# Conditioning products of a first block on TensorE instead of GpSimd, in a two-block transformer kernel on Trainium2

## The chip, the cores and the metric

The kernel runs on one core of one Trainium2 chip. The metric is the device time of one execution in microseconds. Three runs are shown, and their median is what a change is compared with.

## The reference

256 tokens of width 1024 go through two blocks. Both are modulated by conditioning vectors, a product of one activated vector with a wide matrix:

```python
silu_c = jax.nn.silu(c)
mod_lat = jnp.split((silu_c @ w_mod[l] + b_mod[l])[:, None, :], N_MOD, axis=-1)
h_lat = rmsnorm(x, norm_mix_g[l]) * (1 + mod_lat[1]) + mod_lat[0]
mix_lat, mix_ctx = token_mixer(h_lat, h_ctx, ...)
x = x + mod_lat[2] * mix_lat
h_lat = rmsnorm(x, norm_ffn_g[l]) * (1 + mod_lat[4]) + mod_lat[3]
x = x + mod_lat[5] * moe_ffn(h_lat, ...)
...
c_act = jax.nn.silu(c)
mod = c_act @ w_ada[l] + b_ada[l]
shf, scf = jnp.split(c_act @ w_ada_f + b_ada_f, 2, axis=-1)
```

`w_mod` and `w_ada` are 1024 x 6144 in float32, `w_ada_f` is 1024 x 2048. Block 1's `token_mixer` projects the 256 tokens and 256 context tokens with `w_in` (1024 x 9280), runs a gated linear recurrence over both directions (8 heads of 128) and an attention with compressed keys (8 heads), and merges the two through gates. An expert layer follows (32 experts, the best four per token, about 400 MB of weights). Block 2 has another recurrence, a gated scan, a hierarchical expert layer and the last norm. All is float32.

## The kernel before

One core does everything in one program. Weights come from HBM in tiles of 128 x 2048 float32 (1 MB, `wload`, L293). In block 1 a tile of projection weights `w` is split by `wsplit` (L542) into two float32r parts: a cast on ScalarE (`wsh`, L538) and a subtraction on VectorE (`wsl`, L539), in halves of 1024 columns. `mm3` (L548) then multiplies split weights with split activations `hs` in three passes (L551 to L553) into PSUM tiles `tp`, `fp` or `pf`.

TensorE's work is a list of items `self.q`. An item has `prep()`, which issues its weight loads and splits, and `run()`, a generator that issues a few products and yields their time. `step` (L494) prepares the first two items and advances the first; `fill(us)` (L512) steps for so many microseconds, `need` steps until an item is done. The chain of the recurrence for a pair of heads (`chain`, L752) is a generator that issues its own steps on VectorE, ScalarE and TensorE (`gram`, `st`, `av`) and, after each, `fill`s with items: the projections of the next pair of heads. There are four pairs; beside the fourth come the query and key projections, and then the eight gate projections `g8s` (L900). Instructions of one engine run in the order in which the program ends up placing them, and a load is issued where its ring has a slot.

The conditioning vectors are handled as 28 rows of 512 values, and their results are kept in `rowall` (128 x 128; value 128g + i of row r is on partition 32g + r, column i). The four rows that block 1's first norm needs are made on TensorE at the start (`mod_first`, L362): for each of 8 blocks of 128 channels and each of 4 column blocks, a matmul with 32 weight columns (`cpad`, in which the column of row r holds the activated vector and the others zeros) writes 32 partitions of `modps`, a VectorE instruction adds it to `rowall`, and a transpose (`modT`) turns it into columns.

The next twenty rows, `MODS1` (8 of `w_mod`, 12 of `w_ada`), run on GpSimd beside the projections (`pool_mods`, L404). GpSimd issues their loads itself, into two slots of a ring of their own (`wm`). For each half of a row's matrix:

```python
nc.gpsimd.tensor_mul(w4, w4, self.cs[:, c + 4 * a:c + 4 * a + 4, None].to_broadcast([128, 4, 512]))
nc.gpsimd.tensor_add(w[:, 0:1024], w[:, 0:1024], w[:, 1024:2048])
```

and then 512-column sums into `macc` (L434 to L437). `tick` (L476) advances this by one step per `PACE1` = 2800 ns of accounted TensorE work, and 5000 ns after a row's last sum `reduce` (L416) has TensorE add up the partitions: four matmuls against a one-hot column (`mr`, L419), and a VectorE addition to `rowall` (L421). `end_mods` (L442) finishes whatever is left as block 1 ends. The four rows of `w_ada_f` are made later, in block 2, on TensorE by `mod` (L346). `mod_cols` (L396) and `bcast_rows` (L450) turn rows into columns or spread them over partitions.

Of the kernel before, what the change touches and what calls it, by code (L numbers as in the profile page):

```python
# [21 lines left out]
PACE1 = 2800  # L22
MODS1 = [(1, j) for j in range(4, 12)] + [(2, j) for j in range(12)]
NWS, NU, NV = 8, 32, 20
NWR, NWM = 3, 2
# [42 lines left out]
def shape_consts():  # L68
# [16 lines left out]
    c['fconst'] = np.ascontiguousarray(np.concatenate([ident, perm, tri, cosT, sinT, iota], 1))  # L85
# [21 lines left out]
def layout(i):  # L107
# [3 lines left out]
    for n, k in VECS:  # L111
# [13 lines left out]
    d['bmods'] = np.ascontiguousarray(np.concatenate([mix, i['b_mod'][0][2048:], i['b_ada_2'][0], i['b_ada_f_2'], mix])  # L125
                                      .reshape(32, 4, 128).transpose(1, 0, 2).reshape(128, 128))
# [36 lines left out]
class Item:  # L163
    """a piece of work for the tensor engine: prep() starts its loads, run(weights) yields the time of each step"""
# [6 lines left out]
class Router:  # L171
    """logits of x's rows, normed and modulated, as x's columns come in: r * (x @ (A w)) + (B @ w + b)"""
# [17 lines left out]
    def cols(self, j):  # L190
        """columns 256 j .. 256 j + 255 are there"""
# [22 lines left out]
    def finish(self, lgt):  # L214
        """lgt[b]: where the logits go; returns 1 / root mean square of the rows"""
# [10 lines left out]
class Ker:  # L226
# [9 lines left out]
    def run(self):  # L236
        with ExitStack() as es:
            tc = self.tc
            self.cp = es.enter_context(tc.tile_pool(name="const", bufs=1))
            self.wp = es.enter_context(tc.tile_pool(name="wts", bufs=NWM))  # L240
            self.sm = es.enter_context(tc.tile_pool(name="small", bufs=2))
            self.pp = es.enter_context(tc.tile_pool(name="psum", bufs=8, space=PSUM))
            self.q, self.lags, self.side, self.sums = [], [], None, []
            own = self.own = [(self.wp, "w"), (self.wp, "wm")]
# [8 lines left out]
            else:  # L253
# [4 lines left out]
                for _ in self.pool_mods([(2, j) for j in range(12)] + [(3, j) for j in range(4)], lambda n: self.cp.tile([128, 512], F32, name=n, tag=n)):  # L258
                    self.drain()
                self.tick(6000)  # L260
# [7 lines left out]
            if self.start <= 1:  # L268
                with tc.tile_pool(name="moe1", bufs=1, side="right", reuse_waits="tile") as p, tc.tile_pool(name="w2", bufs=NW2, reuse_waits="tile") as wp2, tc.tile_pool(name="w2x", bufs=NW2X, reuse_waits="tile") as wp3:
                    self.wq = own[1:] * 2 + own[:1] * 3 + [(wp3, "w")] * NW2X + [(wp2, "w")] * NW2  # L270
                    self.moe1(p, route, (wp2, "w"))
# [7 lines left out]
            with tc.tile_pool(name="moe2", bufs=1, reuse_waits="tile") as p, tc.tile_pool(name="w2b", bufs=NW2B, reuse_waits="tile") as wp2:  # L279
                self.wq = own[1:] * 2 + own[:1] * 3 + [(wp2, "w")] * NW2B  # L280
# [5 lines left out]
    # ---- helpers  # L286
# [6 lines left out]
    def wload(self, src, n=WCOL, slot=None, eng=None):  # L293
        pool, tag = slot or self.wq[self.wi % len(self.wq)]
        t = pool.tile([128, WCOL], F32, name="w", tag=tag, bufs=NWR if tag == "w" and pool is self.wp else None)
# [8 lines left out]
    def consts(self):  # L304
# [3 lines left out]
        fc = cp.tile([128, 1152], F32, name="fc")  # L308
        nc.scalar.dma_start(fc[:, 0:128], d['fconst'][:, 0:128])
        self.fc_rest = lambda: nc.sync.dma_start(fc[:, 128:], d['fconst'][:, 128:])  # L310
        self.ident, self.perm, self.tri = fc[:, 0:128], fc[:, 128:256], fc[:, 256:384]
        self.cosT, self.sinT, self.iota = fc[:, 384:640], fc[:, 640:896], fc[:, 896:1152]
# [4 lines left out]
        # conditioning vectors: columns for the products with w_mod, w_ada  # L317
# [6 lines left out]
        # views [:, 31-r:63-r] have the filled columns in r and, for the second conditioning, 28+r  # L324
# [4 lines left out]
        self.onehot = cp.tile([128, 63], F32, name="onehot")  # L329
        nc.gpsimd.memset(self.onehot, 0.0)  # L330
        nc.gpsimd.memset(self.onehot[:, 31:32], 1.0)
        # chunks of conditioning vectors: row r's 128 columns of group g on partition 32g+r; biases to begin with
        self.rowall = cp.tile([128, 128], F32, name="rowall")
        nc.scalar.dma_start(self.rowall, d['bmods'])
# [7 lines left out]
    def msrc(self, which, j):  # L342
        src, r, c = {1: ('wmod', j, 0), 2: ('wada', 12 + j, 16), 3: ('wadaf', 24 + j, 16)}[which]
        return [self.d[src][2 * j + a] for a in range(2)], r, c

    def mod(self, which, j, cpad):  # L346
        """work item: a chunk of the conditioning vectors, c@W[:, 512j:512j+512]"""
        nc = self.nc
        src, r, _ = self.msrc(which, j)
# [12 lines left out]
    def mod_first(self, q, tile):  # L362
        """channels 256 q .. 256 q + 255 of block 1's first shift and scale, of both conditionings"""
        nc = self.nc

        def run(ws):
            ps = self.ps("modps")
            for k in range(8):
                for g in range(4):
                    w = ws[g // 2]  # L370
                    w, o = (w[k // 2], 256 * (k % 2)) if isinstance(w, list) else (w, 256 * k)
                    o += 128 * (g % 2)
                    nc.tensor.matmul(ps[32 * g:32 * g + 32, :128], self.cpad1[:, k, 31 - q:63 - q], w[:, o:o + 128],
                                     start=(k == 0), stop=(k == 7))
                yield 210
            nc.vector.tensor_add(self.rowall, self.rowall, ps[:, :128])
            pt = self.ps("modT")
            nc.tensor.transpose(pt[:, :128], self.rowall, self.ident)
            for i, r in enumerate((q, 28 + q)):
                nc.vector.tensor_copy(self.mcol1[:, i, :16].rearrange("p (s k) -> p s k", s=2)[:, :, 2 * q:2 * q + 2],  # L380
                                      pt[:, :128].rearrange("p (s g r) -> p s g r", s=2, g=2)[:, :, :, r])

        def load():
            ws = []
            for s in range(2):
                src = self.d['wmix'][4 * s + q]
                if 2 * q + s < 3:
                    ws.append(self.wload(src, slot=self.own[1 if q == 0 else 0]))
                    continue
# [5 lines left out]

    def mod_cols(self, *todo):  # L396
        """rows to columns: (first row, number, destination [128, 4 n])"""
        nc = self.nc
        pt = self.ps("modT")
        nc.tensor.transpose(pt[:, :128], self.rowall, self.ident)  # L400
        for r, n, dst in todo:
            nc.vector.tensor_copy(dst.rearrange("p (j g) -> p g j", g=4), pt[:, :128].rearrange("p (g r) -> p g r", g=4)[:, :, r:r + n])

    def pool_mods(self, todo, acc_tile):  # L404
        """the same on GpSimd, a step at a time beside the tensor engine's work, which then sums the partitions"""
        nc = self.nc
        slot = (self.wp, "wm")
        loads = [(w, j, a) for w, j in todo for a in range(2)]

        def load(i):  # L410
            if i < len(loads):
                w, j, a = loads[i]
                return self.wload(self.msrc(w, j)[0][a], slot=slot, eng=nc.gpsimd)
# [1763 lines left out]
```

## Time and profile before

| | us |
|---|---|
| runs | 2249.55, 2257.85, 2250.76 |
| median of the runs | 2250.76 |
| profiled execution, first to last instruction (span) | 2246.4 |
| between that span and the median | 4.4 |
| TensorE (PE) busy | 2001.8 (89%) |
| VectorE (DVE) busy | 1133.6 (50%) |
| ScalarE (ACT) busy | 530.4 (24%) |
| GpSimd (POOL) busy | 436.1 (19%) |

The profiled execution is listed with its span alone; its own time is not told apart from the runs'. Block 1 takes the first 645 us or so, its experts the next 1000, and block 2 the rest. In the rows further down, PE is TensorE, DVE VectorE, ACT ScalarE, POOL GpSimd, SP the engine that issues loads. A group of instructions reads: line, engine, operation, output and input by the program's names, their shapes, count | busy time in us, mean ns of one | idle time ahead of them and what ended it.

### The profile page before, as it was taken

What the parts mean: (1) busy time and instruction counts of PE and PEld (TensorE: products, weight loads), DVE (VectorE), ACT (ScalarE), POOL (GpSimd) and SP (SyncE); (2) the same over time, 40 slices, a digit from 0 to 9 for tenths busy, and PEclk for the clock granted to TensorE, in tenths of its full rate; (3) what the DMA queues carried; (4) which work ended last, traced back from release to release, by engine and by line L of the source; (5) the groups of instructions that cost most, each with busy time, mean ns of one, the idle gap of its engine ahead of it and who ended that gap; (6) DMA issues with size and microseconds to landing.
All of it is one profiled execution on the core that took longest, in us unless ns stands there. A gap on an engine that the chain in (4) does not pass through costs nothing. (4 is left out here: it accounts for less than half of the span.)

```text
span 2246.4 us, 31459 instructions
## 1 busy us (share of the span) xinstructions
PE 2001.8 (89%) x13205; PEld 1202.1 (54%) x13206; DVE 1133.6 (50%) x1766; ACT 530.4 (24%) x925; POOL 436.1 (19%) x245
## 2 busy tenths in 40 slices
PE   6578779889989999998999999999969998898996
PEld 4467668776674333333333333333348998765653
DVE  5987998997552323333332424233368564321223
ACT  3233335424341000000000100000035633221112
POOL 1754755996300000000000000000032201000000
PEclk9698989989999999998999999999979999899998
DMA  8333424554369999999999999999942236799992
GB/s 340 120 124 130 136 100 151 187 199 167 132 256 374 417 418 416 419 410 387 416 418 418 416 416 417 417 416 418 373 179 99 77 120 257 262 367 337 363 357 78
DMA packets 172908, 646.11 MB, mean 288 GB/s; under 512 B 11508, under 2 KB 78068, under 8 KB 125524
## 3 DMA queue, kind: packets, MB, share of 16 engines
q1 hardware_dynamic: 165216, 600.84, 68.9%
q0 software_dynamic: 5760, 41.95, 5.3%
q8 instruction: 108, 1.77, 0.3%
q10 hardware_dynamic: 1780, 1.20, 0.2%
q14 instruction: 44, 0.36, 0.0%
HBM read 642.89 MB, written 1.05 MB: 287 GB/s over the span
## 5 line engine op out<-in xcount | busy, mean ns | idle before, releaser
L1307 PE MATMUL gu<-w,gT 128*64 128x512 f32 x2048 | 480.8, 596 | 0.0
L1307 PEld LDWEIGHTS gu<-w,gT 128*64 128x64 f32 x2048 | 147.6, 137 | 277.0 <-issue 260.3
L539 DVE TENSOR_TENSOR wsl<-w,wsh 128x1024 fp32r<-128x1024 f32 (+1 forms) x141 | 242.6, 1735 | 46.5 <-ACT wsh L538 46.3
L1338 PE MATMUL y<-w,aT 128*64 128x512 f32 x1024 | 229.7, 600 | 0.1
L1774 POOL MEMSET cpad<- 128x504 f32 x1 | 0.5, 517 | 1059.5 <-DVE x L1239 1059.5
L538 ACT CAST wsh<-w 128x1024 fp32r<-128x1024 f32 (+1 forms) x141 | 143.7, 1028 | 209.2 <-PE tp L552 150.9
L1317 DVE TENSOR_SCALAR act<-gu 128x256 f32<-128x256 f32 x64 | 27.2, 425 | 310.6 <-PE gu L1376 307.3
L1222 DVE SCALAR_TENSOR_TENSOR ylo<-y,sw,yhi 128x512 fp32r<-128x512 f32 x64 | 48.1, 751 | 254.0 <-ACT yhi L1221 254.0
L429 POOL TENSOR_TENSOR w<-w,cs 128x2048 f32<-128x2048 f32 x40 | 154.7, 3867 | 25.6 <-DMA w<-in_wmod_dram 14.8
L553 PE MATMUL tp<-hs,wsl 128*128 128x256 f32 (+1 forms) x424 | 143.6, 339 | 11.8 <-DVE wsl L539 11.7
L1338 PEld LDWEIGHTS y<-w,aT 128*64 128x64 f32 x1024 | 72.9, 138 | 148.1 <-issue 143.3
L551 PE MATMUL tp<-hs,wsh 128*128 128x256 f32 (+1 forms) x424 | 149.9, 353 | 0.2 <-DVE sg L898 0.2
L552 PE MATMUL tp<-hs,wsh 128*128 128x256 f32 (+1 forms) x424 | 142.5, 336 | 0.0
L1481 PE MATMUL ab<-w,gT 128*64 128x256 f32 x1024 | 127.7, 385 | 0.0
L1221 ACT ACTIVATE yhi<-y,sw 128x512 fp32r<-128x512 f32 x64 | 44.0, 687 | 293.4 <-PE y L1376 239.7
L431 POOL TENSOR_TENSOR w<-w 128x1024 f32<-128x1024 f32 x40 | 109.2, 2732 | 2.8
L1238 DVE TENSOR_TENSOR gated<-co,gtb 128x512 f32<-128x512 f32 x128 | 88.4, 690 | 33.7 <-PE co L1233 26.3
L1319 ACT ACTIVATE sge<-act 128x512 f32<-128x512 f32 x32 | 20.2, 631 | 351.0 <-DVE act L1317 351.0
L553 PEld LDWEIGHTS tp<-hs,wsl 128*128 128x128 f32 x424 | 89.8, 212 | 19.3 <-DVE wsl L539 13.4
L1481 PEld LDWEIGHTS ab<-w,gT 128*64 128x64 f32 x1024 | 76.4, 137 | 39.1 <-issue 8.3
L551 PEld LDWEIGHTS tp<-hs,wsh 128*128 128x128 f32 x424 | 90.2, 213 | 7.7 <-issue 2.7
L552 PEld LDWEIGHTS tp<-hs,wsh 128*128 128x128 f32 x424 | 90.0, 212 | 5.3 <-issue 1.0
(562 smaller groups left out, 3733.6 us busy)
## 6 DMA issues: line engine op xcount, KB each, us to landing
w<-in_wgu_dram SPq DMA_DIRECT2D x256, 1024.0 KB, 15.3
w<-in_wdn_dram SPq DMA_DIRECT2D x128, 1024.0 KB, 15.8
w<-in_win_dram SPq DMA_DIRECT2D x50, 1024.0 KB, 4.9
w<-in_w1e_dram SPq DMA_DIRECT2D x32, 1024.0 KB, 9.5
w<-in_w3e_dram SPq DMA_DIRECT2D x32, 1024.0 KB, 10.3
w<-in_w2e_dram SPq DMA_DIRECT2D x32, 1024.0 KB, 10.0
w<-in_wada_dram POOLq DMA_DIRECT2D x24, 1024.0 KB, 5.3
w<-in_wmod_dram POOLq DMA_DIRECT2D x16, 1024.0 KB, 5.2
```

Source lines behind the costliest of these rows:

```text
L429: nc.gpsimd.tensor_mul(w4, w4, self.cs[:, c + 4 * a:c + 4 * a + 4, None].to_broadcast([128, 4, 512]))
L431: nc.gpsimd.tensor_add(w[:, 0:1024], w[:, 0:1024], w[:, 1024:2048])
L538: nc.scalar.copy(hi, src)
L539: nc.vector.tensor_sub(lo, src, hi.bitcast(F32))
L551: nc.tensor.matmul(out, a[0], b[0], start=first, stop=False)
L552: nc.tensor.matmul(out, a[0], b[1], start=False, stop=False)
L553: nc.tensor.matmul(out, a[1], b[0], start=False, stop=last)
L1222: nc.vector.scalar_tensor_tensor(lo, y, w, hi.bitcast(F32), op0=OP.mult, op1=OP.subtract)
L1238: nc.vector.tensor_mul(part, o[s], gate[:, cs])
L1307: nc.tensor.matmul(gu[j][64 * s:64 * s + 64, :], g[:, k, c0:c0 + 64], w[:, 1024 * s + 512 * j:1024 * s + 512 * j + 512], start=(k == 0), s ...
L1338: nc.tensor.matmul(y[64 * s:64 * s + 64, :], aT[:, k % 4, k // 4, :], w[:, o:o + 512], start=(k == 0), stop=False)
L1481: nc.tensor.matmul(ps[64 * j:64 * j + 64, 256 * i:256 * i + 256], g[:, k, c0 + 64 * j:c0 + 64 * j + 64], w[j][:, k, :], start=(k == 0), st ...
```

## The change

The twenty rows become items of TensorE's list. `modrow` makes a row with eight matmuls: the 8 blocks of 128 channels go four at a time to the four groups of 32 columns of the array, 512 values wide, so that `modps` (128 x 512) holds four partial sums of a row, which VectorE adds to a `rowall` that is now 128 x 512 (biases on partitions 0 to 31, zeros below). `fold_rows` adds the four partial sums as it turns rows into columns (four matmuls against `fold`, four stacked unit matrices of 32), and `bcast_rows` does it in one matmul. `mixed` puts one such item behind each projection: four per pair of heads for three pairs, then eight between the gate projections. Their loads go through the same ring as the projections' weights, which has five slots (`NWR`) in place of three and two (`NWM`), and through SP's queue. `pool_mods`, `end_mods`, `PACE1` and the one-hot matrix go. The padded vector for the second conditioning (`cpad2`) is made at the start by GpSimd, and `mod_first` uses `modrow` too.

```diff
-NWR, NWM = 3, 2
+NWR = 5
...
+    def modrow(self, cpad, r, pieces):
+        nc = self.nc
+        ps = self.ps("modps")
+        for o, w in pieces:
+            for h in range(2):
+                for g in range(4):
+                    k = 4 * h + g
+                    wk = w(k)
+                    n = wk.shape[-1]
+                    nc.tensor.matmul(ps[32 * g:32 * g + 32, o:o + n], cpad[:, k, 31 - r:63 - r], wk, start=(h == 0), stop=(h == 1))
+                yield 1.7 * n
+        nc.vector.tensor_add(self.rowall, self.rowall, ps)
...
         def run(ws):
-            ps = self.ps("modps")
-            for k in range(8):
-                for g in range(4):
-                    o = 512 * (k % 4) + 128 * g
-                    nc.tensor.matmul(ps[32 * g:32 * g + 32, :128], cpad[:, k, 31 - r:63 - r], ws[k // 4][:, o:o + 128],
-                                     start=(k == 0), stop=(k == 7))
-                yield 210
-            nc.vector.tensor_add(self.rowall, self.rowall, ps[:, :128])
+            yield from self.modrow(cpad, r, [(0, lambda k: ws[k // 4][:, 512 * (k % 4):512 * (k % 4) + 512])])
         return Item(lambda: [self.wload(t) for t in src], run)
...
+    def fold_rows(self):
+        pt = self.ps("modT")
+        for g in range(4):
+            self.nc.tensor.matmul(pt[:, 32 * g:32 * g + 32], self.rowall[:, 128 * g:128 * g + 128], self.fold, start=True, stop=True)
+        return pt[:, :128]
...
-        self.wq = self.own[:1]
-        self.side = [0, self.pool_mods(MODS1, u), PACE1]
+        mods = [self.mod(*m) for m in MODS1]
+        def mixed(items):
+            out = []
+            for it in items:
+                out.append(it)
+                if mods:
+                    out.append(mods.pop(0))
+            return out
...
-                self.add(*nxt.items, nxt.val)
-                est = 10.3 + 25.6
+                self.add(*mixed([*nxt.items, nxt.val]))
+                est = 10.3 + 25.6 + 6.8
...
-                self.add(*g8s)
+                self.add(*mixed(g8s))
...
         self.drain()
-        self.end_mods()
-        self.wq = self.own
```

Three places in the order of instructions show it. The first is SP's queue, which issues the loads of block 1: `win` are the projections' weights, `wrope` those of the rotary keys, `wqb` those of the queries. Before, from the masks' load (`mk`) on:

```order
L310 DMA fc<-in_fconst_dram 128x1024
L672 DMA mk<-in_masks_dram 128x448 x2
L301 DMA w<-in_win_dram 128x2048 x18
L301 DMA w<-in_wrope_dram 128x1024
L301 DMA w<-in_win_dram 128x2048 x12
L301 DMA w<-in_wqb_dram 128x1536 x2
```

and now, around the start of the gate projections (`wada` are conditioning weights):

```order
L299 DMA w<-in_wada_dram 128x2048 x2
L299 DMA w<-in_win_dram 128x2048 x4
L299 DMA w<-in_wrope_dram 128x1024
L299 DMA w<-in_win_dram 128x2048
L299 DMA w<-in_wada_dram 128x2048 x2
L299 DMA w<-in_win_dram 128x2048
```

The conditioning weights, which GpSimd issued for itself, stand in pairs behind each load of a projection.

The second is TensorE in the second pair of heads, where a row meets the chain's products (`gram`). Before, the same kind of place, the end of a row's sums (`mr`) among projections:

```order
L552 MATMUL tp<-hs,wsh 128x256
L553 MATMUL tp<-hs,wsl 128x256
L419 MATMUL mr<-macc,onehot 32x128 x4
L551 MATMUL tp<-hs,wsh 128x256
L552 MATMUL tp<-hs,wsh 128x256
```

and now:

```order
L497 MATMUL tp<-hs,wsh 128x256
L498 MATMUL tp<-hs,wsl 128x256
L355 MATMUL modps<-w,cpad_87 32x512 x4
L738 MATMUL gram<-cq,ck 128x128 x4
L355 MATMUL modps<-w,cpad_87 32x512 x4
L496 MATMUL fp<-wsh,hs 128x256
```

Four small matmuls give way to eight of 512 columns, here cut in two by the chain's products; 4 of the 20 rows are cut so, the other 16 stand in one piece.

The third is VectorE among the gate projections (`sg` and `s` are gates, `yh` the recurrence's output). Before:

```order
L539 TENSOR_TENSOR wsl<-w,wsh 128x1024 x3
L421 TENSOR_TENSOR rowall<-rowall,mr 128x128
L539 TENSOR_TENSOR wsl<-w,wsh 128x1024
L898 TENSOR_TENSOR sg<-sg,tp 128x512
L899 TENSOR_TENSOR s_3591<-s_3591,sg 128x512
L974 TENSOR_TENSOR yh<-yh,s_3591 128x512
```

and now:

```order
L853 TENSOR_TENSOR s_3528<-s_3528,sg 128x512
L484 TENSOR_TENSOR wsl<-w,wsh 128x1024 x2
L357 TENSOR_TENSOR rowall<-rowall,modps 128x512
L928 TENSOR_TENSOR yh<-yh,s_3528 128x512
L357 TENSOR_TENSOR rowall<-rowall,modps 128x512
L484 TENSOR_TENSOR wsl<-w,wsh 128x1024 x2
```

An addition of 512 columns per row, which waits for the row's matmuls, now stands ahead of the next projection's splits.

## Rows read from the trace of the kernel before

**Rows 1.** The page's 40 slices of 56.2 us: busy tenths, and GB/s moved.
```profile
DVE  5987998997552323333332424233368564321223
...
POOL 1754755996300000000000000000032201000000
...
GB/s 340 120 124 130 136 100 151 187 199 167 132 256 374 417 418 416 419 410 387 416 418 418 416 416 417 417 416 418 373 179 99 77 120 257 262 367 337 363 357 78
```
**Rows 2.** Timeline of SP's queue as block 1 ends: start us, length us, first expert weights.
```profile
645.34 4.26 SPq L301 DMA_DIRECT2D w<-in_wgu_dram  x7
```
**Rows 3.** Windows: stretch, length, busy us by engine, granted clock, DMA share, GB/s.
```profile
52.50:108.00 55.50, 27.87 (x126) 22.78 (x125) 51.85 (x42) 13.38 (x20) 47.05 (x22) 0.69 0.32 114
108.00:427.00 319.00, 257.03 (x1619) 227.57 (x1618) 278.35 (x385) 123.94 (x256) 193.49 (x98) 0.89 0.38 134
427.00:521.00 94.00, 82.02 (x617) 77.56 (x617) 90.99 (x45) 32.80 (x40) 87.82 (x37) 0.93 0.59 212
521.00:640.00 119.00, 110.43 (x672) 80.78 (x670) 72.24 (x118) 47.18 (x88) 44.94 (x23) 0.97 0.34 121
1760.00:1880.00 120.00, 116.55 (x1726) 108.70 (x1724) 65.42 (x92) 57.29 (x72) 9.93 (x9) 1.00 0.38 135
```
**Rows 4.** Waits of PE from 52.5 to 640 us: us in total, times, longest.
```profile
PE ktT L732 <- DVE ex L725: 53.4, 11, 10.6
PE tp L553 <- DVE wsl L539: 11.7, 6, 5.6
```
**Rows 5.** Groups on DVE from 52.5 to 108 us.
```profile
L539 DVE TENSOR_TENSOR wsl<-w,wsh 128x1024 fp32r<-128x1024 f32 x5 | 14.9, 3012 | 2.0 <-ACT wsh L538 2.0
...
L721 DVE TENSOR_TENSOR_SCAN ex<-fs,ones 128x255 f32<-128x255 f32 x2 | 4.8, 2378 | 0.0
...
L724 DVE TENSOR_TENSOR_SCAN ex<-fs,ones 128x255 f32<-128x255 f32 x2 | 1.3, 674 | 0.0
...
L740 DVE SCALAR_TENSOR_TENSOR qT<-tp,qT 128x512 f32<-128x512 f32 x1 | 0.7, 678 | 0.0
```
**Rows 6.** Groups on DVE from 437 to 521 us.
```profile
L539 DVE TENSOR_TENSOR wsl<-w,wsh 128x1024 fp32r<-128x1024 f32 x20 | 54.3, 2752 | 1.9 <-ACT wsh L538 1.9
```
**Rows 7.** Groups on DVE from 1660 to 2000 us, in block 2.
```profile
L539 DVE TENSOR_TENSOR wsl<-w,wsh 128x1024 fp32r<-128x1024 f32 x48 | 59.4, 1248 | 23.9 <-ACT wsh L538 23.8
```
**Rows 8.** Groups on DVE from 52.5 to 521 us.
```profile
L798 DVE COPY_PREDICATED att<-masks,gram 128x256 f32<-128x256 uint8 x56 | 22.4, 438 | 4.2 <-PE gram L790 4.0
```
**Rows 9.** Groups on POOL from 40 to 640 us.
```profile
L429 POOL TENSOR_TENSOR w<-w,cs 128x2048 f32<-128x2048 f32 x40 | 154.7, 3867 | 25.6 <-DMA w<-in_wmod_dram 14.8 <-DMA w<-in_wada_dram 10.7
L431 POOL TENSOR_TENSOR w<-w 128x1024 f32<-128x1024 f32 x40 | 109.2, 2732 | 2.8
L434 POOL TENSOR_TENSOR macc<-w 128x512 f32<-128x512 f32 x20 | 34.0, 1702 | 125.4 <-DVE ex L725 22.2 <-PE ktT L732 20.2 <-DVE qsl L539 17.7
L437 POOL TENSOR_TENSOR macc<-macc,w 128x512 f32<-128x512 f32 x20 | 30.2, 1510 | 1.6
L436 POOL TENSOR_TENSOR macc<-macc,w 128x512 f32<-128x512 f32 x20 | 26.8, 1340 | 0.5
```
**Rows 10.** Timeline of PE, a row of the head, and a chain's product: start us, us.
```profile
49.79 1.95 PE L373 MATMUL modps<-wmx,cpad 128*32 128x128 f32 x64
51.68 0.50 PE L551 MATMUL pf<-hs,wsh 128*128 128x512 f32 x1
52.01 0.40 PE L552 MATMUL pf<-hs,wsh 128*128 128x512 f32 x1
52.25 0.39 PE L553 MATMUL pf<-hs,wsl 128*128 128x512 f32 x1
...
118.86 1.05 PE L790 MATMUL gram<-cq,ck 128*128 128x128 f32 x8
119.66 0.48 PE L551 MATMUL tp<-hs,wsh 128*128 128x512 f32 x1
```
**Rows 11.** The page's loads: engine's queue, count, KB each, median us to landing.
```profile
w<-in_win_dram SPq DMA_DIRECT2D x50, 1024.0 KB, 4.9
```

More of the change, by code (lines that the diff above doesn't have):

```diff
@@ L257, in run @@
                 self.nc.sync.dma_start(self.x1, self.d['xin'])
-                for _ in self.pool_mods([(2, j) for j in range(12)] + [(3, j) for j in range(4)], lambda n: self.cp.tile([128, 512], F32, name=n, tag=n)):
-                    self.drain()
-                self.tick(6000)
+                self.add(*(self.mod(2, j) for j in range(12)))
+                self.drain()
                 self.mod_cols((12, 10, self.mcol2[:, 0:40]))
@@ L294, in wload @@
         pool, tag = slot or self.wq[self.wi % len(self.wq)]
-        t = pool.tile([128, WCOL], F32, name="w", tag=tag, bufs=NWR if tag == "w" and pool is self.wp else None)
+        t = pool.tile([128, WCOL], F32, name="w", tag=tag, bufs=None)
         if slot is None:
@@ L366, in run, with piece @@
         def run(ws):
[L367 to L378, printed above, removed]
+            def piece(w):
+                return lambda k: w[k // 2][:, 256 * (k % 2):256 * (k % 2) + 256] if isinstance(w, list) else w[:, 256 * k:256 * k + 256]
+            yield from self.modrow(self.cpad1, q, [(256 * s, piece(w)) for s, w in enumerate(ws)])
+            pt = self.fold_rows()
             for i, r in enumerate((q, 28 + q)):
                 nc.vector.tensor_copy(self.mcol1[:, i, :16].rearrange("p (s k) -> p s k", s=2)[:, :, 2 * q:2 * q + 2],
-                                      pt[:, :128].rearrange("p (s g r) -> p s g r", s=2, g=2)[:, :, :, r])
+                                      pt.rearrange("p (s g r) -> p s g r", s=2, g=2)[:, :, :, r])
         def load():
@@ L387, in load @@
                 if 2 * q + s < 3:
-                    ws.append(self.wload(src, slot=self.own[1 if q == 0 else 0]))
+                    ws.append(self.wload(src))
                     continue
@@ L404, in pool_mods @@
[L404 to L413, printed above, removed]
-        ws = [load(0), load(1)]
-        def reduce(r, acc):
-            ps = self.ps("mr")
-            for g in range(4):
-                nc.tensor.matmul(ps[32 * g:32 * g + 32, :128], self.onehot[:, 31 - r:63 - r], acc[:, 128 * g:128 * g + 128],
-                                 start=True, stop=True)
-            nc.vector.tensor_add(self.rowall, self.rowall, ps[:, :128])
-        for n, (which, j) in enumerate(todo):
-            _, r, c = self.msrc(which, j)
-            acc = acc_tile("macc")
-            for a in range(2):
-                w = ws[a]
-                w4 = w.rearrange("p (k n) -> p k n", k=4)
-                nc.gpsimd.tensor_mul(w4, w4, self.cs[:, c + 4 * a:c + 4 * a + 4, None].to_broadcast([128, 4, 512]))
-                yield
-                nc.gpsimd.tensor_add(w[:, 0:1024], w[:, 0:1024], w[:, 1024:2048])
-                yield
-                if a == 0:
-                    nc.gpsimd.tensor_add(acc, w[:, 0:512], w[:, 512:1024])
-                else:
-                    nc.gpsimd.tensor_add(acc, acc, w[:, 0:512])
-                    nc.gpsimd.tensor_add(acc, acc, w[:, 512:1024])
-                ws[a] = load(2 * n + 2 + a)
-                yield
-            self.sums.append([5000, lambda a=(r, acc): reduce(*a)])
@@ L442, in end_mods @@
-    def end_mods(self):
-        for _ in self.side[1] if self.side else ():
-            pass
-        self.side = None
-        for s in self.sums:
-            s[1]()
-        self.sums = []
+            self.nc.vector.tensor_copy(dst.rearrange("p (j g) -> p g j", g=4), pt.rearrange("p (g r) -> p g r", g=4)[:, :, r:r + n])
     def bcast_rows(self, keys, dst, last=None):
@@ L455, in bcast_rows @@
             r = self.msrc(*key)[1]
[L456 to L458 removed]
+            nc.tensor.matmul(ps, self.fold[:, r:r + 1].to_broadcast([128, 128]), self.rowall, start=True, stop=True)
             (last or nc.scalar.copy)(o, ps)
@@ L601, in block1 @@
             if q == 0:
-                raw = [(self.wload(win[4 + 4 * i], slot=self.own[0]),) for i in range(2)]
+                raw = [(self.wload(win[4 + 4 * i]),) for i in range(2)]
         self.fc_rest()
+        rc = p.tile([128, 640], F32, name="rc")
+        nc.sync.dma_start(rc, d['fconst'][:, 544:])
+        self.perm, self.cosT, self.sinT = rc[:, 0:128], rc[:, 128:384], rc[:, 384:640]
         masks = p.tile([128, 7 * 128], U8, name="masks")
```

74 lines of the change are left out of this document (28 added, 46 removed).

## The prediction, made before the change was run

> **What bounds the kernel now.** I read the page's slices first. VectorE is at nine tenths in much of the first quarter and GpSimd is busy there and almost nowhere else [rows 1]. From slice 14 to 28 the last row stays near 416 GB/s but for two dips: that is the first expert stage, which streams weights, and what is done about block 1 cannot shorten it. The weight loads of that stage start together as block 1 ends, at 645 us [rows 2], so a microsecond that block 1 gives up moves everything behind it by a microsecond.
>
> Next the windows [rows 3]. From 52.5 us (the first projection) to 640 us there are 587.5 us, in which TensorE is busy for 27.9 + 257.0 + 82.0 + 110.4 = 477.3. So it is idle for 110.2. Its granted clock is 0.69, 0.89, 0.93 and 0.97 in the four stretches, which are means over its two levels of 1.2 and 2.4 GHz. Busy time times what is missing to 1 gives what the lower level costs: 8.6 + 28.3 + 5.7 + 3.3 = 45.9. I call the sum, 156.1 us, the excess: 36.3 in 52.5 to 108, 90.3 in 108 to 427, 17.7 in 427 to 521, 11.9 in 521 to 640. What is left, 431.4 us, is TensorE's own need: 19.2, 228.7, 76.3 and 107.1. The last row of the same group is a stretch of block 2 with the same way of queueing work and hardly any GpSimd: 3.45 us idle in 120 and a clock of 1.00, an excess of 2.9%.
>
> The waits then say who causes the idle time: mostly TensorE waiting for VectorE's products of forget gates and for split weights [rows 4]. And VectorE is slow there, not overloaded by its own work: the low half of a weight split takes 3.01 us and one scan 2.38 us, where the mirrored scan of the same size takes 0.67 [rows 5]; with GpSimd busy for 87.8 of 94 us the split takes 2.75 [rows 3, 6], with GpSimd nearly idle 1.25 [rows 7]. The masked copy, one of whose operands lies in PSUM, takes 0.44 beside a busy GpSimd [rows 8]. So what bounds block 1 is that VectorE and GpSimd wait for each other, and TensorE for VectorE. GpSimd's five groups of products and sums for the 20 conditioning rows are 154.7 + 109.2 + 34.0 + 30.2 + 26.8 = 354.9 us [rows 9]. The Trainium skill ("SBUF — State Buffer", section "Who interferes with whom") has a rule for this: the two engines share a pair of ports, and a VectorE instruction with two inputs in SBUF contends with a GpSimd one that reads there. The trace agrees: 2.75 against 1.25 us for the split, and 0.44 for the masked copy.
>
> **The change, part by part.** *GpSimd's arithmetic goes.* The 354.9 us of it, and its 40 loads' issues, leave an engine for which only VectorE and the sums waited. What that frees is the excess, and I price it by stretch. In 52.5 to 108 VectorE is busy 51.85 us. At free speed its groups come to some 22: five splits at 1.25 are 6.2 instead of 14.9, the long scans 1.3 instead of 4.8, the other twenty instructions of 256 to 512 columns at 0.4 to 0.7 [rows 5, 7]. TensorE's need there is 19.2, and the two alternate only in part. I take 28 us for the stretch, 9 above the need: **27.5 saved**. In 108 to 427 three pairs of heads each run a chain of gate products through ScalarE, VectorE and TensorE with projections as filler. VectorE was busy for 278 of 319 us; at some 180 free (the ratio of splits and scans) it is no longer the longest, and I leave 20 of the 90.3 of excess, two and a half times the rate of block 2. In 427 to 521 I leave 9 of 17.7, in 521 to 640 5.5 of 11.9. Left in all: 43.5. The bounds are 14.6, the rate of block 2 over some 505 us, and the whole 156.1.
>
> *The rows come to TensorE.* In the trace the first four rows ran there already: 64 records from 49.79 to the next product's start at 51.68, which is 1.89 us, and that product's successor came 0.33 later where the usual spacing is 0.24 [rows 10]. The new form passes the same number of columns through the same rows, 512 at a time, so I take 1.95 a row. Ends: 1.9 and 2.3, the latter if each row also disturbs its neighbours as the old sums seem to. Twenty rows are **39 us added**: 23.4 in the pairs, 15.6 among the eight gate projections at the end of the stretch to 521. That all lies on the path, since TensorE is what remains. Four rows in the pairs are cut in two by a chain's product, as the excerpt of TensorE's order shows. The Trainium skill ("TensorEngine Tiling (Array Packing)", Tiling Modes, Key Properties) says that a change of tiling mode drains the engine, which speaks against strewing such rows among projections. The trace agrees so far as it can: at the 0.10 of eight 128-column records [rows 10] and four groups at once, 64 records would be 1.6 us and not 1.89, so 0.29 is what a row pays for entry and exit. By that rule the four cut rows would pay it again, 1.2 us, and the sum would come out one later; my sum goes by the uncut row.
>
> *The old sums go*: 20 groups of eight records, 0.2 us each at 0.10 a record and four at once [rows 10], **4 saved**.
>
> *VectorE's add per row* widens from 128 to 512 columns: 0.68 by the product of that shape from PSUM [rows 5], 20 times, 13.6 in place of some 6. In the pairs it lies beside TensorE. In the last three gate projections it stands right ahead of a split, which the cover there (a projection of 48 products, 5.8 us at half of the 0.24 spacing) still hides. Cost nothing, 1.7 us each at worst if that cover is short, 5 in all; this is inside the 9 that I leave.
>
> *The loads move to SP's queue*, 40 MB of them, in order behind the projections' weights, with five slots in one ring in place of three and two. A 1 MB load lands in 4.9 us [rows 11]. By TensorE's order a slot comes free at least one projection and one row ahead of its need, 7.7 us, so load, cast and split (4.9, 1.25 by the split and as much for the cast, an estimate) just fit. Among the eight gate projections 3 MB are wanted in each such period: 25.2 MB at 416 GB/s [rows 1] are 60.5 us against 8 x 7.75 = 62 us of TensorE. It is even, and this is why I leave 9 us there. In the pairs the demand is half of it and hidden.
>
> *The head and the small ones.* The four first rows' adds widen, and four small products replace one transpose, each time with VectorE and TensorE waiting for one another: **2 added**. Broadcasts get one wide product in place of four narrow; the padded vector is made early; block 2's four rows use the new form at the same work. Nothing.
>
> By stretch: 52.5 to 108 becomes 28 (27.5 saved). 108 to 427 becomes 228.7 - 2.6 + 23.4 + 20 = 269.5 (49.5 saved). 427 to 521 becomes 76.3 - 0.9 + 15.6 + 9 = 100 (6 added). 521 to 640 becomes 107.1 - 0.5 + 5.5 = 112 (7 saved). With the head's 2: 27.5 + 49.5 - 6 + 7 - 2 = **76 saved**. The span becomes 2170.4; what lay around it, 4.4 to the median, stays. **Forecast 2175 us.**
>
> **The rivals.** *Half of the chains' excess stays.* The chain is a series of steps through three engines, and GpSimd may be only half of why it is late; TensorE's wait for gate products, 53.4 us, is the largest [rows 4]. For it: even a free VectorE must follow TensorE and ScalarE. Against it: filler is queued, and block 2 gets by with 2.9%. 35 of the 70 that I take from the pairs would stay: 2210. *All of it stays*: 2245, which is no change, 0.5% or 11 us being about what a measurement of this kernel can tell.
>
> *The loads come too late, and it is slower.* A row is in TensorE's order, so if its 2 MB are late, everything queued behind waits; before, GpSimd's lateness held up nobody. The place is each of 20 rows; the price is a load, a cast and a split exposed, about 7.3 us, 146 in all: 2321. It decides from 3.8 us per row on (76 / 20). Against it stands the 7.7 us of lead and five slots; for it, that the lead just equals the need and the transfers run at the ceiling in one stretch.
>
> *VectorE is slow for another reason*, say traffic of the loads. Then the 112.6 of excess I take stays: 2175 + 113 = 2288. Against it: the masked copy is not slowed, and the splits of block 2 run at 1.25 with DMA as busy (0.38 in both [rows 3]).
>
> *The column groups do not run together at 512 columns.* Then a row takes 64 x 0.10 = 6.4: 20 x 4.45 = 89 more, 2264. The 128-column form shows them together.
>
> **How the numbers follow.** Chances: forecast 0.76, half of the chains' excess stays 0.12, all of it 0.05, late loads 0.04, another reason 0.02, groups in series 0.01. The forecast and the half make faster, 0.88; all of the excess makes no change, 0.05; the last three make slower, 0.07. The range: 29 us better with the excess of block 2, 2146, and 2142 with a head and sums that cost less than I take; at the other end 2210 for the half, and 7 more with rows at 2.3: 2218.
>
> **What would show it.** Right: the splits near 1.25 us throughout block 1 and the scans near 0.67; GpSimd empty up to 600 us; the first product of a chain near 81 us instead of 108, where the first window ends; rows on TensorE 1.9 to 2.1 us apart from what follows; 416 GB/s touched among the gate projections; block 1 ending near 569 instead of 645. Wrong: TensorE waiting for the conditioning weights' transfer or for casts behind it (late loads), a clock still under 0.95 in the pairs with TensorE waiting for gate products (chain), splits still over 2 us (another reason), or the expert stage growing by what block 1 loses.

## The result and the profile after

The changed kernel takes 2143.98 us (median of four runs, 2139.77 to 2147.53) against 2250.16 on the same chip: a ratio of 0.953, 95% interval 0.951 to 0.955, **106 us faster**. Forecast were 2175 us and a range from 2142 to 2218. The profiled execution spans 2145.4 us, 101.0 less than the one before.

The slices of the page after, in the form of [rows 1]:

```profile
DVE  5666664454323332333323332333476646322223
...
POOL 0000000000000000000000000000132101000000
...
GB/s 356 79 221 192 236 128 272 259 88 81 338 413 424 422 424 422 355 307 424 424 424 425 425 423 425 423 425 425 337 62 85 108 125 263 311 370 253 378 382 110
```

GpSimd is all but empty until block 2 (it is busy for 3.8 us before the fourth row), and in the first quarter VectorE is down from nine tenths to six or less, though it does the same work and wider additions. The windows of the changed kernel, cut at five events near the bounds of [rows 3] (fourth row's start, first `gram` product of a chain, last one, first product of the attention's keys, end of block 1):

```profile
54.40:84.40 30.00, 26.48 (x176) 22.86 (x176) 21.14 (x47) 13.30 (x20) 0.00 (x0) 0.89 0.22 76
84.40:331.00 246.60, 246.60 (x1661) 206.29 (x1660) 159.31 (x381) 116.69 (x249) 0.00 (x0) 1.00 0.48 178
331.00:431.90 100.90, 96.74 (x770) 81.95 (x769) 46.63 (x54) 37.99 (x47) 0.00 (x0) 1.00 0.73 282
431.90:540.40 108.50, 107.66 (x638) 78.94 (x637) 50.43 (x110) 47.96 (x89) 0.00 (x0) 1.00 0.25 85
```

The second number is the length, the third TensorE's busy time. In the chains TensorE is now busy for all of 246.60 us at a granted clock of 1.00, the higher of the two levels (2.4 GHz); before, it was busy for 257 of 319 at 0.89. Idle time and lost clock, reckoned as in the prediction, are 6.4 + 0 + 4.2 + 0.8 = 11.4 us, down from 156.1 (155.4 with the kernel before cut at the same five events). The largest waits of TensorE from 50 to 580 us, against those of [rows 4]:

```profile
PE tp L498 <- DVE wsl L484: 4.1, 3, 1.6
...
PE ktT L680 <- DVE ex L671: 1.4, 1, 1.4
```

And the groups of VectorE in that stretch:

```profile
L484 DVE TENSOR_TENSOR wsl<-w,wsh 128x1024 fp32r<-128x1024 f32 x79 | 95.5, 1222 | 66.2 <-ACT wsh L483 66.1
L746 DVE COPY_PREDICATED att<-masks,gram 128x256 f32<-128x256 uint8 x56 | 23.1, 445 | 7.9 <-PE gram L738 7.8
L357 DVE TENSOR_TENSOR rowall<-rowall,modps 128x512 f32<-128x512 f32 x21 | 14.4, 686 | 22.7 <-PE modps L355 22.6
...
L672 DVE TENSOR_TENSOR_SCAN ex<-fs,ones 128x255 f32<-128x255 f32 x8 | 5.5, 684 | 0.0
L669 DVE TENSOR_TENSOR_SCAN ex<-fs,ones 128x255 f32<-128x255 f32 x8 | 5.5, 682 | 0.0
```

The split takes 1.22 or 1.23 us in each of the four stretches, both scans 0.68, and the masked copy what it took before.

By stretch, from the timelines of the two profiled executions in us (the products of a chain are `gram` here; the last one starts at 420.9 before, not at the 427 of the prediction's window):

| stretch | before | after | change | forecast |
|---|---|---|---|---|
| to the fourth row on TensorE | 49.8 | 54.4 | +4.6 | +2 |
| to the first product of a chain | 58.7 | 30.0 | -28.7 | -27.5 |
| to the chains' last product | 312.4 | 247.4 | -65.0 | -49.5 |
| to the first product of keys | 100.3 | 100.1 | -0.2 | +6 |
| to the end of block 1 | 123.7 | 108.5 | -15.2 | -7 |
| to the end | 1601.5 | 1605.0 | +3.5 | 0 |
| sum | 2246.4 | 2145.4 | -101.0 | -76 |

The medians differ by 106.2 us and these spans by 101.0, because the profiled execution of the changed kernel is the slowest of its four (2147.53 us).

### The profile page after: what moved, and what is told of

It reads as the page before. It is cut to its first block, busy times and chain, and to the rows that moved or that the text cites. A ratio compares the mean times of both kernels' runs of the same rounds, so it can differ in the third digit from the quotient of the medians.

```text
span 2145.4 us, 30927 instructions
## 1 busy us (share of the span) xinstructions
PE 2007.2 (94%) x13008; PEld 1181.0 (55%) x13009; DVE 920.8 (43%) x1766; ACT 528.8 (25%) x925; POOL 60.3 (3%) x66
## 5 line engine op out<-in xcount | busy, mean ns | idle before, releaser
L484 DVE TENSOR_TENSOR wsl<-w,wsh 128x1024 fp32r<-128x1024 f32 (+1 forms) x141 | 168.7, 1209 | 99.3 <-ACT wsh L483 99.1
L483 ACT CAST wsh<-w 128x1024 fp32r<-128x1024 f32 (+1 forms) x141 | 143.3, 1030 | 163.5 <-PE tp L497 108.5
L496 PE MATMUL tp<-hs,wsh 128*128 128x256 f32 (+1 forms) x424 | 139.7, 330 | 0.0
L498 PE MATMUL tp<-hs,wsl 128*128 128x256 f32 (+1 forms) x424 | 134.4, 317 | 4.1 <-DVE wsl L484 4.1
L497 PE MATMUL tp<-hs,wsh 128*128 128x256 f32 (+1 forms) x424 | 133.7, 315 | 0.0
L1215 PE MATMUL ga<-oh,xhi 128*128 128x256 f32 x256 | 77.5, 330 | 15.4 <-DVEq L1229 6.2
L496 PEld LDWEIGHTS tp<-hs,wsh 128*128 128x128 f32 x424 | 81.7, 193 | 16.3 <-issue 4.9
L1191 DVE TENSOR_TENSOR x<-x,gated 128x512 f32<-128x512 f32 x128 | 88.2, 689 | 3.2
L498 PEld LDWEIGHTS tp<-hs,wsl 128*128 128x128 f32 x424 | 81.8, 193 | 9.9 <-DVE wsl L484 4.9
L496 PE MATMUL tp<-hi,wsh 128*128 128x256 f32 x288 | 86.5, 300 | 0.0
L497 PEld LDWEIGHTS tp<-hs,wsh 128*128 128x128 f32 x424 | 81.8, 193 | 4.5 <-issue 0.7
```

Of the source, the lines that this page charges most:

```text
L483: nc.scalar.copy(hi, src)
L484: nc.vector.tensor_sub(lo, src, hi.bitcast(F32))
L496: nc.tensor.matmul(out, a[0], b[0], start=first, stop=False)
L497: nc.tensor.matmul(out, a[0], b[1], start=False, stop=False)
L498: nc.tensor.matmul(out, a[1], b[0], start=False, stop=last)
L1191: nc.vector.tensor_add(x[:, b, cs], x[:, b, cs], part)
```

## The experiments

**GpSimd's arithmetic beside the changed kernel.** The edit, with GpSimd's steps placed by the old accounting of TensorE's work:

```diff
+        ju = p.tile([128, 1000], F32, name="ju")
...
+        def busy():
...
+                    for _ in range(2):
+                        nc.gpsimd.tensor_mul(ju, ju, self.cs[:, 4 * a:4 * a + 1].to_broadcast([128, 1000]))
+                    yield
+                    for _ in range(2):
+                        nc.gpsimd.tensor_add(ju[:, 0:500], ju[:, 0:500], ju[:, 500:1000])
...
+        self.side = [0, busy(), 2800]
```

> The changed kernel with GpSimd doing, at the old pace of one step per 2800 ns of accounted TensorE work, as many products and sums on a tile of zeros as it did before (20 rows); nothing reads that tile. Theory (GpSimd's reads of SBUF hold up VectorE, VectorE holds up TensorE): splits in block 1 near 2 us again, and most of the excess of before comes back, 100 to 145 us, so 2245 to 2290 us. Rival (what went was GpSimd's own lateness, its loads or the waits on its sums): nobody waits for this work, so 2144 to 2155 us and splits at 1.22.

It took 2317.6 us, a ratio to the kernel before of 1.029 (1.027 to 1.032), 174 us more than the changed kernel and more than the theory's upper end. Its windows, and VectorE's group of splits from 52.5 to 390 us and from 400 to 620 us:

```profile
30.00:150.00 120.00, 63.22 (x312) 44.78 (x313) 96.53 (x84) 21.39 (x34) 114.82 (x71) 0.71 0.22 80
150.00:250.00 100.00, 59.71 (x316) 47.46 (x316) 100.00 (x93) 23.20 (x51) 95.53 (x58) 0.78 0.22 82
250.00:390.00 140.00, 106.63 (x651) 85.06 (x649) 134.70 (x123) 37.89 (x79) 133.88 (x79) 0.85 0.37 136
390.00:500.00 110.00, 102.73 (x672) 85.29 (x673) 76.27 (x171) 57.19 (x120) 5.30 (x4) 0.95 0.44 158
```
```profile
L490 DVE TENSOR_TENSOR wsl<-w,wsh 128x1024 fp32r<-128x1024 f32 x25 | 49.3, 1991 | 0.4 <-ACT wsh L489 0.4
...
L490 DVE TENSOR_TENSOR wsl<-w,wsh 128x1024 fp32r<-128x1024 f32 x43 | 51.8, 1221 | 29.7 <-ACT wsh L489 29.6
```

The fifth number is VectorE's busy time, the seventh GpSimd's. Nothing waits for this work, and yet as long as it lasts the split takes 1.99 us, VectorE is busy for 80 to 100% of a window, TensorE is idle for over a third of the time and its mean clock is 0.71 to 0.85; when it ends, the split is back at 1.22 and the clock at 0.95. The rival falls. The size was off because I had taken the pace from the old kernel. There GpSimd's groups stood idle for 25.6 us ahead of products, for loads, and for 125.4 us ahead of a row's first sums [rows 9]. Here its instructions wait for no other engine, so that placing them by TensorE's work does not spread them: they ran almost without a break from 5 to 395 us, 372 us of them in place of 354.9, and the first product of a chain came at 152.3 us instead of 84.4. That this early run makes the difference in size is likely and was not tested.

**GpSimd that only writes.** The same places with `nc.gpsimd.memset(ju, 0.0)`, eight or nine fills of 1000 columns for each half row.

> The same, but GpSimd only fills a tile with zeros, about as long in all. Theory that it is GpSimd's reading that collides with VectorE's second SBUF operand: splits at 1.22 us, time 2144 to 2160. Rival (any GpSimd access to SBUF blocks VectorE): splits near 2 us and over 2220 us.

2154.2 us, ratio 0.957 (0.955 to 0.960): 10 us over the changed kernel, which is near the noise (0.957 against 0.953); in the profiled executions 6 of them lie ahead of the first product of a chain. The groups of GpSimd from 20 to 340 us, of VectorE's splits from 52.5 to 300 us and of its `tensor_scalar` from 20 to 340 us, and then that last group in the changed kernel (50 to 580 us) to compare:

```profile
L795 POOL MEMSET ju<- 128x1000 f32 x152 | 142.7, 939 | 8.7
...
L490 DVE TENSOR_TENSOR wsl<-w,wsh 128x1024 fp32r<-128x1024 f32 x34 | 41.1, 1219 | 14.3 <-ACT wsh L489 14.1
...
L680 DVE TENSOR_SCALAR f<-fs,lb 128x256 f32<-128x256 f32 x16 | 17.6, 1101 | 0.0
```
```profile
L674 DVE TENSOR_SCALAR f<-fs,lb 128x256 f32<-128x256 f32 x16 | 6.5, 408 | 0.0
```

The fills stand at three lines of the program, of which the first group is one; together they keep GpSimd busy for 292 of 310 us (seventh number of the window):

```profile
30.00:340.00 310.00, 298.92 (x1988) 244.52 (x1981) 218.39 (x461) 139.13 (x286) 292.21 (x313) 0.98 0.48 178
```

With GpSimd writing all this time the split is not slowed at all (1.22), but the operation with one tensor and two column scalars is: 1.10 us instead of 0.41. The three other groups of `tensor_scalar` on 256 columns are slowed as well, to 0.74, 0.71 and 0.52 us from 0.41, 0.41 and 0.27; the four cost VectorE 25 us more in all. So the split, which has two SBUF inputs, is held up by GpSimd's products and sums and not by its fills, which only write, while `tensor_scalar` is held up by fills too. The Trainium skill ("SBUF — State Buffer", "Who interferes with whom") has both parts: a VectorE instruction with two SBUF inputs contends with a GpSimd one that reads there and not with one that only writes, and `tensor_scalar` can enter a mode that uses both ports, in which it contends with GpSimd. The trace agrees with the first (1.99 and 1.22 us); of the second it shows the slowing, and no run shows in which mode these instructions ran. Little of VectorE's work here is `tensor_scalar`, which fits 10 us and not 174.

**The kernel before without GpSimd's products and sums.**

```diff
-                nc.gpsimd.tensor_mul(w4, w4, self.cs[:, c + 4 * a:c + 4 * a + 4, None].to_broadcast([128, 4, 512]))
...
-                nc.gpsimd.tensor_add(w[:, 0:1024], w[:, 0:1024], w[:, 1024:2048])
...
+                nc.gpsimd.tensor_copy(acc[:, 256 * a:256 * a + 256], w[:, 0:256])
```

> The kernel before without GpSimd's products and sums: each row's partial sums are replaced by two copies of 256 columns, so the conditioning rows are not computed; its loads through GpSimd's queue, TensorE's sums and VectorE's additions stay. Theory: the excess goes and no rows are on TensorE, so the changed kernel less 39 us plus 4 for the old sums: about 2109 us. Rival (the loads through GpSimd's queue, or waits on the sums, slowed block 1): 2230 to 2255.

2107.7 us, ratio 0.937 (0.934 to 0.940). The theory said 2109. The loads of 40 MB through GpSimd's queue are still there, and the split takes 1.23 us (VectorE's group from 52.5 to 540 us, and the loads issued from 77 to 390 us):

```profile
L533 DVE TENSOR_TENSOR wsl<-w,wsh 128x1024 fp32r<-128x1024 f32 x79 | 96.9, 1229 | 67.3 <-ACT wsh L532 66.7
...
w<-in_wada_dram POOLq DMA_DIRECT2D x22, 1024.0 KB, 7.2
w<-in_wmod_dram POOLq DMA_DIRECT2D x10, 1024.0 KB, 6.0
```

So neither the loads nor their queue slowed block 1; the arithmetic did, and it cost 141 us. The rows are wrong in this version, but the experts still took 935.9 us from their first `gu` product to the last, against 934.5, so that the total can be read. The same number says what the changed kernel pays for the rows: 2144.0 - 2107.7 = 36 us. Of the 40.0 us between the two profiled executions 7.1 lie ahead of the first product of a chain, 17.7 in the chains and 20.3 among the gate projections; behind these the changed kernel is 5.1 faster.

**The rows, narrow.** The matmuls of the twenty rows take 16 columns, `ws[k // 4][:, 512 * (k % 4):512 * (k % 4) + 16]`; VectorE's addition covers the same 16, and loads and order stay.

> The changed kernel with the twenty rows' matmuls 16 columns wide instead of 512 (the rest of each row is left out); loads, waits and order stay. Theory (TensorE is the bound of block 1 and the rows lie on the path): 20 x 1.7 us less, about 2110. Rival (the rows fill waits and cost little): 2135 to 2147.

2381.0 us, ratio 1.058 (1.054 to 1.061). The total says nothing: with the rows wrong, the experts were chosen otherwise, some got more tokens than the main path holds, and the expert stage made 2240 of its `gu` products instead of 2048 and took 1196 us instead of 935. Block 1, which comes ahead of that, can be read. The chains took 228.3 us instead of 247.4, which is 19.1 us or 1.6 per row. The stretch after them took 100.2 us, **as long as with full rows**:

```profile
82.60:311.00 228.40, 228.33 (x1669) 205.36 (x1667) 153.06 (x381) 116.62 (x250) 0.00 (x0) 1.00 0.53 194
311.00:411.20 100.20, 90.11 (x762) 86.10 (x761) 42.89 (x54) 37.66 (x47) 0.00 (x0) 0.91 0.73 281
```

TensorE was idle for 10 us there and its mean clock was 0.91. In the chains the rows are on the path, among the gate projections something else is just as long.

**The rows without their loads.** They read a resident tile, `rc[:, 0:512]`, and enter with a factor of 1e-5.

> The changed kernel with the twenty rows' matmuls reading one resident tile instead of loaded weights, so the 40 loads are left out and the rows are not computed (their values enter scaled to almost nothing); the routing of the experts changes with them, so only block 1 is to be read. Theory (among the gate projections the 3 MB per projection and row are the bound, elsewhere the loads are hidden): from the last product of the chains to the first product of keys 95 us instead of 100, the rest of block 1 within 2 us of the changed kernel. Rival (TensorE is the bound there as well): 100 us there too. If loads contend everywhere, the pairs of heads get faster as well, by over 5 us.

The stretch took 95.2 us, the chains 247.4 as before (one execution, 2141.6 us):

```profile
84.30:331.70 247.40, 247.40 (x1667) 207.10 (x1666) 160.11 (x382) 117.49 (x251) 0.00 (x0) 1.00 0.22 77
331.70:426.90 95.20, 95.13 (x763) 80.94 (x761) 45.73 (x53) 37.41 (x46) 0.00 (x0) 1.00 0.35 119
```

With the loads and hardly any matmuls of the rows the stretch takes 100.2, with the matmuls and no loads of the rows 95.2, and then TensorE is busy throughout. So among the gate projections it is the loads that bound the changed kernel, by 5 us, while in the chains the same loads are hidden to the last tenth. The theory holds. Whether the transfers' rate or the number of slots is behind these 5 us was not told apart: the stretch moved 281 GB/s at a DMA share of 0.73, and SP's queue spent 89 of its 100 us waiting for the splits and rows that free a slot (its waits in the changed kernel from 331.8 to 431.9 us):

```profile
SPq L299 <- DVE wsl L484: 45.7, 13, 5.4
SPq L299 <- PE modps L355: 43.0, 16, 7.0
```

The kernel before without GpSimd's arithmetic has no rows on TensorE in these two stretches, and issues conditioning loads from GpSimd's queue into two slots of their own, eight of them in the second stretch:

```profile
77.30:307.00 229.70, 229.70 (x1578) 205.96 (x1577) 156.34 (x382) 118.43 (x251) 25.08 (x48) 1.00 0.50 186
307.00:386.80 79.80, 79.80 (x657) 76.93 (x656) 42.19 (x48) 36.57 (x46) 9.24 (x16) 1.00 0.69 262
```

TensorE never stands idle there. Against 79.8 us the 95.2 are 15.4 us more for eight rows, 1.9 each.

**Four slots.** `NWR = 4`.

> The changed kernel with four slots in the ring of weights instead of five (the experts' rings have one slot less too). The rival of the prediction, loads that come too late for a row in TensorE's order, is a matter of how far ahead a slot comes free: with a slot less it should show, with TensorE waiting for splits or rows, 10 to 60 us slower than the changed kernel, most of it among the gate projections. If the lead of five was ample, 2144 to 2150.

2170.2 us, ratio 0.963 (0.958 to 0.968), 26 us more than with five. But the chains took 247.4 us again; of the 21.8 us between the two profiled executions 8.1 came at the head, where TensorE waits once for a first row's weights, 5.2 among the gate projections and 5.0 among the experts. TensorE's waits from 20 to 560 us:

```profile
PE modps L355 <- DMA w<-in_wmix_dram: 9.3, 1, 9.3
PE tp L498 <- DVE wsl L484: 8.4, 5, 2.2
```

Late loads as a rival needed 3.8 us for each row; even a slot less doesn't do that. The expectation of the size was right, that of the place wrong: among the gate projections were 5.2 of the 21.8 us.

**Where else the rows could go.** Two edits follow from this: spread the last eight rows, or take four rows that only block 2's end needs out of block 1, to the start of block 2. There TensorE waits 19.7 us for the norm in the changed kernel:

```profile
PE xT L1603 <- DVE xh L1576: 19.7, 1, 19.7
```

```diff
-MODS1 = [(1, j) for j in range(4, 12)] + [(2, j) for j in range(12)]
+MODS1 = [(1, j) for j in range(4, 12)] + [(2, j) for j in range(8)]
...
+        rest = [self.mod(2, j) for j in range(8, 12)]
+        for it in rest[:2]:
+            it.ready, it.w = True, it.prep()
         ahead = [(self.wload(win2[2 + j]),) for j in range(2)]
+        self.add(*rest)
...
+        self.drain()
         h, hm, hs = [], [], []
```

> The changed kernel once more, as the measure for the next three on the same chip: 2144 us, ratio 0.953.

> The changed kernel with four of block 2's twelve rows moved out of block 1 to the start of block 2, where TensorE waits about 20 us for the norm; four rows are left among the eight gate projections, behind every second one. Theory (the gate projections lose 20 us to eight rows and their 16 MB, the wait at block 2 is free and its loads find slots): 8 to 10 us faster than the changed kernel, about 2135. Rival (the rows' loads push back those of block 2's projections): no gain, 2142 to 2150.

> The changed kernel with the last eight rows spread over all twelve gate projections (five among the first eight, three among the four that run beside the attention, where DMA is busy a quarter of the time). Theory (loads bound the eight projections): about 4 us faster, 2140. Rival (only TensorE counts): 2144 as before.

> Both: four rows at the start of block 2, three among the eight gate projections and one beside the attention. Theory: as with four rows late, perhaps 1 us more, 2134. Rival: no difference from the changed kernel.

On one chip, ratios to the kernel before: the changed kernel 0.952 (0.950 to 0.953), 2142.4 us; four rows late 0.946 (0.945 to 0.948), **2130.5 us**; spread alone 0.950 (0.949 to 0.952), 2139.4, which is inside the noise; four late and spread 0.948 (0.947 to 0.950), 2134.0, so that spreading adds nothing to four rows late. In the traces spreading alone takes the stretch among the gate projections from 100.1 to 95.0, what it took without loads; all eight rows still lie in it and TensorE is busy throughout, so the mechanism shows though the total can't tell it:

```profile
329.60:424.60 95.00, 95.00 (x762) 80.91 (x762) 45.41 (x53) 37.38 (x46) 0.00 (x0) 1.00 0.77 296
```

With four rows late the stretch is 87.1, 13.0 less than in the changed kernel, and TensorE is busy throughout there too:

```profile
330.00:417.10 87.10, 87.03 (x699) 79.12 (x698) 43.44 (x49) 37.17 (x46) 0.00 (x0) 1.00 0.63 226
```

At the start of block 2 it costs 2.2 us (to the first product with `lora` weights), since two of the four rows come in late (timeline of TensorE in that version, with idle time and releaser at the end):

```profile
1523.35 3.64 PE L355 MATMUL modps<-w,cpad 128*32 128x512 f32 x32 [0.32 <-DVE gated L1193]
1540.47 1.93 PE L355 MATMUL modps<-w,cpad 128*32 128x512 f32 x8 [13.48 <-DMA w<-in_wada_dram]
1544.19 1.94 PE L355 MATMUL modps<-w,cpad 128*32 128x512 f32 x8 [1.79 <-DMA w<-in_wada_dram]
```

> Six of block 2's rows at its start instead of four, two among the eight gate projections. Theory: the gate projections are bound by TensorE with four rows among them, so two fewer give 3.9 us; the 20 us of waiting at block 2 hold six rows of TensorE's work (11.7 us), but 12 MB of loads ahead of the projections' weights push these back by 4 us or more: within 3 us of the version with four, 2128 to 2133. Rival (the wait still hides all of it): 2126 or less.

> The version with four rows late, as the measure for the one with six on the same chip: 2130.

Six rows late took 2146.6 us, ratio 0.953 (0.951 to 0.956), four of them again 2132.4, 0.948 (0.946 to 0.949). Both the theory and its rival missed. The gate projections gained 4.1 us, but the start of block 2 lost 11.7, where TensorE now stood through seven waits for rows' weights (its waits from 1470 to 1600 us):

```profile
PE modps L355 <- DMA w<-in_wada_dram: 20.6, 7, 12.5
```

These two make a loss of 7.6 of the 15.2 us between the two profiled executions; most of the rest lies further on in block 2, and why is open. A wait of 20 us has room for six rows on TensorE, and not for their 2 MB each: DMA moved 349 GB/s around it with four rows and 375 with six. The version with four rows late beats both kernels, by 0.5% over the changed one.

## Why the prediction was right

The direction, the mechanism and, in every stretch of block 1 but one, the sign were right; the gain was 106 us where I forecast 76. That the time still lies in the range, by 2 us, is near luck: the low end of 2142 stood on a head and sums cheaper than I took, but the head cost more, and two of the four executions lie below it.

- *What bounds the kernel.* Right. The excess was GpSimd's doing: 156.1 us reckoned from idle time and clock, 141 us when only GpSimd's arithmetic is taken away, 11.4 left after the change.
- *What would be left of the excess* is the step that failed in size. I put it as 43.5 (9 + 20 + 9 + 5.5); it was 11.4 (6.4 + 0 + 4.2 + 0.8). These 32 us are more than the 25 by which the spans miss; the head and the part behind block 1 took 6 more than forecast. The 20 in the chains were a guess that TensorE would still wait for the chain's own steps; [rows 4] showed 53.4 us of such waits, and all of it was VectorE held up, none the chain's length: the kernel before without GpSimd's arithmetic has no rows on TensorE as filler, and still TensorE is busy for all of the chains' 229.7 us. The upper of my own bounds on the gain, the excess of block 2 at 2.9%, would have given 14.6.
- *The 4.4 us from span to median* make the other 6 us of the miss. They set one execution against the median of others and are no cost of their own: here the same difference is -1.4, and within one execution it is 2.1 (2147.5 against 2145.4).
- *The price of a row.* 1.95 us forecast; 1.85 in the timeline (105.61 to 107.46 below), 1.9 among the gate projections by the run without loads. The changed kernel pays 36 us in all, where I forecast 35 for twenty rows less the old sums, but that they agree so well is in part chance: the 36 hold 7.1 ahead of the chains and the 5 of loads, and the 5.1 gained behind the gate projections.

```profile
105.61 1.92 PE L355 MATMUL modps<-w,cpad 128*32 128x512 f32 x16
107.46 1.16 PE L738 MATMUL gram<-cq,ck 128*128 128x128 f32 x8
...
132.47 1.07 PE L355 MATMUL modps<-w,cpad 128*32 128x512 f32 x8
133.47 1.16 PE L738 MATMUL gram<-cq,ck 128*128 128x128 f32 x8
134.56 1.06 PE L355 MATMUL modps<-w,cpad 128*32 128x512 f32 x8
135.56 0.39 PE L496 MATMUL fp<-wsh,hs 128*128 128x256 f32 x1
```

- *A row cut in two* takes 1.00 + 1.00 us, 0.15 more than a whole one (one of each, above), so cutting made a difference of some 0.6 us for four rows, half of the 1.2 that I worked out.
- *The even fight among the gate projections*, 60.5 us of loads against 62 of TensorE, was called right in that neither wins by much: the loads do, by 5 us. But my 416 GB/s were not what the stretch ran at, 281 on average. The 9 left there were 4.2.
- *The last part of block 1* gave 15.2 instead of 7. GpSimd's 44.9 us of work there [rows 3] cost more than I gave it, but 3.4 of the 15.2 are not GpSimd's arithmetic: from the first product of keys to the experts' first, the kernel before takes 156.3 us, without that arithmetic 145.7, and the changed one 142.3.
- *The head* cost 4.6 instead of 2. Between equal programs this varies by a microsecond or two (first product of a chain at 83.6 and 84.4 in two executions of the changed kernel, at 82.6 and 85.0 in two of the version with four rows late).
- *The rivals.* Late loads: they cost 5 us among the gate projections with five slots and 26 in all with four, where the rival wanted 146 and needed 76 to decide. Another reason for VectorE's slowness: ruled out by the experiments with and without GpSimd's arithmetic. Groups in series: ruled out, a row would take 6.4. Excess that stays in the chains: none did.
- *The expert stage* I called bound by its transfers at 416 GB/s. It moved at 424 after the change, paused in slices 17 and 18, and took 935.2 us from its first product to its last against 934.5. TensorE sets its length: it is busy for 906 of 936 us there, and none of its waits there is for a load. This changed nothing in the sum.

## What to carry to other kernels

An engine that nobody waits for can still be the one that decides, if its instructions slow down another engine's: compare one instruction's mean time with the neighbour busy and idle (here 2.75 and 1.25 us) before calling an engine busy. When this hold-up went, 145 of the 156 us of idle time and lost clock downstream of it went too; price what remains by a stretch of the same kernel that never had it (block 2's rate gave 14.6 us, and 11.4 remained). And a work item that moves into another engine's order brings its transfers along: look in each stretch whether time or bytes fill first.

## What the hardware showed unexpectedly

GpSimd filling memory at 94% of the time left a two-input VectorE instruction at 1.22 us and took one group of `tensor_scalar` on 256 columns from 0.41 to 1.10. And the granted TensorE clock stayed at the higher level from 79.5 us to the end of block 1, 461 us, once the waits were gone, where before it fell to the lower one (1.2 GHz) sixteen times between 52.5 us and the end of block 1, for 3 to 21 us each.
